# Gate and up weights of a pair of column blocks, read by depth halves in runs of 1 KB

## The chip, the core and the metric

The kernel runs on one core of one Trainium2 chip. The metric is the device time of one execution in microseconds (us), the median of three runs. The reference is float32 in and out.

## The reference

One layer of a decoder trunk, for a sequence of 1024 rows of width 1024. The change touches the two feed-forward blocks, one at the start and one at the end of the layer:

```python
def swiglu(h, w_gate, w_up, w_down):
    return (jax.nn.silu(h @ w_gate) * (h @ w_up)) @ w_down
...
x = x + 0.5 * swiglu(rms_norm(x, g_ffn1[l]), w1_gate[l], w1_up[l], w1_down[l])
h = rms_norm(x, g_mix[l])
proj = h @ w_in[l]
...   # two kinds of attention on proj, gates, an output projection added to x
x = x + 0.5 * swiglu(rms_norm(x, g_ffn2[l]), w2_gate[l], w2_up[l], w2_down[l])
```

`w_gate` and `w_up` are 1024 x 2816, `w_in` is 1024 x 4104, all float32. A row of a gate or up matrix is 11264 bytes.

## The kernel before, in words

**Tiling.** `ffn_in` computes gate and up for 22 column blocks of 128 columns, taken in 11 pairs `p`. For each pair the gate matrix (`e` = 0) and the up matrix (`e` = 1) each give a 256 x 1024 left side, cut into four quarters of 128 columns by 512 depth rows: A11, A12 (first block, first and second half of the depth), A21, A22 (second block). The first pair is multiplied directly (`opening`). Every later pair goes through seven products in place of eight (Strassen's scheme, `products`), so that four sums of quarters are formed first (`left_sides`: s1 to s4, on VectorE). Each left operand is then split into a rounded high part and a rest (`halve`: ScalarE copies to fp32r, GpSimd subtracts), and each product is twelve matmuls (`times`).

**Loads.** A load brings 512 KB into one `raw` tile of 128 partitions x 1024 float32. Before the change a load is one column block over the whole depth: 8 depth blocks x 128 columns, so each run in the weight matrix is 128 floats (512 bytes). The tile's first half is then A11 (or A21), its second half A12 (or A22). Four `raw` buffers go in turn: two for gate, two for up. The loads for a pair are issued as soon as the buffers of the pair before come free. In profile and order the tiles are `a0r` and `a1r` (gate and up of the first feed-forward block, the "a block") and `b0r`, `b1r` (of the last one, the "b block"); the high and low parts have names such as `a04A` and `a04S` (pair 4, gate).

**Work beside the a block.** While the a block runs, the kernel also splits columns of `w_in` into high and low parts for later: 48 pieces, each a load `swr` (256 KB, runs of 512 bytes, L799), a ScalarE copy `swh` (L789), a VectorE subtraction (L790) and two stores such as `wg14hd` and `wg14ld` (L793). Three pieces are under way at a time. `behind` ties each step of a piece to the end of one of the seven products, so that they follow TensorE's pace; their tiles are reused in turn, so that a new `swr` load waits for an older store to have landed. The b block has no such work beside it.

**What sets the order.** A scheduler puts the instructions of each engine in order when the program is built; VectorE's and ScalarE's instructions in `products` follow the products. All loads and stores here are issued by SyncE (SP) on one queue, in one order, and each waits until the eighth issue before it has landed (the waits on `DMAHW0` to `DMAHW7` below), besides the waits for its buffer.

**On ScalarE and VectorE** the steps of a piece stand in the same in-order queues as the steps that TensorE needs. In `products`, the accumulator `pd` is read by VectorE (L491, into `u3`) before the last product may add to it, and the accumulator `pa` of the next matrix is copied by ScalarE (L481) before it is added to. A piece's `swh` or subtraction that stands ahead of these in its queue and waits for a transfer holds them up.

Of the kernel before, what the change touches and what calls it, by code (L numbers as in the profile page):

```python
# [16 lines left out]
AF = mybir.ActivationFunctionType  # L17
# [40 lines left out]
def f32(ap):  # L58
    return ap.bitcast(F32)
# [186 lines left out]
def trunk(ctx, tc, x, positions, g_ffn1, w1_gate, w1_up, w1_down, g_mix, w_in, g_cq, w_uq_a, w_q_idx,  # L246
# [128 lines left out]
    def halve(t, src, eng=None):  # L375
# [2 lines left out]
        (eng or nc.gpsimd).tensor_tensor(t[:, LO], src, f32(t[:, HI]), op=ALU.subtract)  # L378
        return t

    class Right:


# [51 lines left out]
                nc.vector.tensor_sub(out[j], a[j], b[j])  # L435

    def loader(raw, nm):
        def load(w, f, name):
            t = raw(name)
            nc.sync.dma_start(t.rearrange("p (k f) -> p k f", k=ND),  # L440
                              w[0, :, f * P:(f + 1) * P].rearrange("(k p) f -> p k f", p=P))
            return t

        return load

    def ffn_in(nm, R, wg, wu, raw, op, sums, ct, bank, staged, rows, first=None, beside=lambda n, ins: None):

        B, load = R.B, loader(raw, nm)  # L450

        def left_sides(rs, name, pinned):
            A11, A12, A21, A22 = (r[:, q] for r in rs for q in (HI, LO))
            O = {n: op(f"{name}{n}") for n in ("A11", "S2", "S3", "S1", "A12", "A22", "S4")}
            s1, s2, s3, s4 = (sums(f"{name}s{n}") for n in range(1, 5))
            in_turn_ = tc.keep_in_program_order if pinned else lambda i: i
            in_turn_(nc.vector.tensor_add(s1, A21, A22))
            in_turn_(nc.vector.tensor_sub(s2, s1, A11))
            in_turn_(nc.vector.tensor_sub(s3, A11, A21))
            in_turn_(nc.vector.tensor_sub(s4, A12, s2))  # L460
            for n, src in (("A11", A11), ("S2", s2), ("S3", s3), ("S1", s1), ("A12", A12), ("A22", A22), ("S4", s4)):
                halve(O[n], src)
            return O

        def times(a, b, ps, start=True):
            for k in range(4):
                c, l = slice(k * P, (k + 1) * P), slice(512 + k * P, 512 + (k + 1) * P)
                nc.tensor.matmul(ps, a[:, c], b[k][:, HI], start=start and k == 0, stop=False, skip_group_check=True)  # L468
                nc.tensor.matmul(ps, a[:, c], b[k][:, LO], start=False, stop=False, skip_group_check=True)  # L469
                ins = nc.tensor.matmul(ps, a[:, l], b[k][:, HI], start=False, stop=k == 3, skip_group_check=True)  # L470
            return ins

        def mul(O, n, ps, start=True):
            a, b = FACTORS[n]
            beside("1675243".index(str(n)), times(O[a], B[b], ps, start))

        def products(O, name, nxt):
            pa = bank("pa", "a")
            mul(O, 1, pa)
            u2 = ct(f"{name}u2")  # L480
            nc.scalar.activation(u2, pa, AF.Copy)  # L481
            pb = bank("pb", "b")
            mul(O, 6, pb)
            nc.vector.tensor_add(u2, u2, pb)
            pc = bank("pc", "c")
            mul(O, 7, pc)
            u3 = ct(f"{name}u3")
            nc.vector.tensor_add(u3, u2, pc)
            pd = bank("pd", "d")
            mul(O, 5, pd)  # L490
            tc.keep_in_program_order(nc.vector.tensor_add(u3, u3, pd))  # L491
            nxt = nxt()
            mul(O, 2, pa, False)
            mul(O, 4, pc, False)
            c21 = ct(f"{name}c21")
            nc.vector.tensor_add(c21, u2, pc)
            mul(O, 3, pd, False)
            nc.vector.tensor_add(u2, u2, pd)
            return (pa, u2, c21, u3), nxt

        def opening(raws, rows, nxt):


            A = [dict(zip(("A11", "A12", "A21", "A22"), (r[:, q] for r in rs for q in (HI, LO)))) for rs in raws]
            O = ({}, {})

            def left(e, *names):
                for n in names:
                    O[e][n] = halve(op(f"{nm}{e}0{n}"), A[e][n])

            ps, sg = {}, {}

            def half(e, r, c, q):

                letter = "abcd"[r + 2 * c]
                if not q:
                    ps[e, r, c] = bank(f"p{letter}", letter)
                times(O[e][f"A{r + 1}{q + 1}"], B[f"B{q + 1}{c + 1}"], ps[e, r, c], not q)

            def gate(r, c):  # L520
                sg[r, c] = ct(f"{nm}sg")
                nc.scalar.activation(sg[r, c], ps[0, r, c], AF.Silu)

            def gated(r, c):
                nc.vector.tensor_mul(sg[r, c], sg[r, c], ps[1, r, c])

            if "B11" not in B:
                left(0, "A11")
                R.operand("B12")
                R.turn("B11")  # L530
                left(0, "A12")
                R.turn("B21")
                left(0, "A21", "A22")
                R.second()
            else:
                left(0, "A11", "A12", "A21", "A22")
            for t, n in enumerate(("A11", "A12", "A21", "A22")):
                if 4 - t <= len(rows):
                    R.stat(rows[t + len(rows) - 4])
                left(1, n)  # L540
            for t in rows:
                R.norm(t)
            half(0, 0, 0, 0)
            half(0, 0, 0, 1)
            gate(0, 0)
            half(0, 1, 0, 0)
            half(0, 1, 0, 1)
            gate(1, 0)
            half(1, 0, 0, 0)
            R.turn("B12", "cd")  # L550
            half(1, 0, 0, 1)
            R.sum("T1")
            gated(0, 0)
            R.turn("B22", "cd")
            half(1, 1, 0, 0)
            half(1, 1, 0, 1)
            gated(1, 0)
            half(0, 0, 1, 0)
            R.turn("T1", "ab")
            half(0, 0, 1, 1)  # L560
            gate(0, 1)
            R.sum("T2")
            half(0, 1, 1, 0)
            R.turn("T2", "ab")
            half(0, 1, 1, 1)
            gate(1, 1)
            R.sum("T4")
            R.sum("T3")
            half(1, 0, 1, 0)
            half(1, 0, 1, 1)  # L570
            R.turn("T3", "ab")
            gated(0, 1)
            nxt = nxt()
            half(1, 1, 1, 0)
            half(1, 1, 1, 1)
            R.turn("T4", "ab")
            gated(1, 1)
            return [sg[0, 0], sg[0, 1], sg[1, 0], sg[1, 1]], [ct(f"{nm}s{n}") for n in range(3)], nxt

        def silu(c):  # L580
            sg = ct(f"{nm}sg")
            nc.scalar.activation(sg, c[0], AF.Silu)
            for t in c[1:]:
                nc.scalar.activation(t, t, AF.Silu)  # L584
            return sg, *c[1:]

        def finish(p, H, S):
            (a11, a21, a12, a22), (s1, s2, s3) = H, S
            nc.vector.tensor_add(s1, a21, a22)
            nc.vector.tensor_sub(s2, s1, a11)  # L590
            nc.vector.tensor_sub(s3, a11, a21)
            nc.vector.tensor_sub(a21, a12, s2)
            for n, t in enumerate((a11, a12, a22, s1, s2, s3, a21)):
                nc.sync.dma_start(staged[p][n * P:(n + 1) * P, :], t)

        def lefts(p, e, pinned=False):
            if p == NF // 2:
                return None
            return left_sides([load((wg, wu)[e], 2 * p + q, f"{nm}{e}r{p}") for q in range(2)], f"{nm}{e}{p}", pinned)

        for p in range(NF // 2):
            if not p:
                first = first or [[load(w, q, f"{nm}{e}r0") for q in range(2)] for e, w in enumerate((wg, wu))]
                with tc.manual_schedule(engines={e.engine for e in (nc.tensor, nc.vector, nc.scalar, nc.gpsimd)}):
                    H, S, nxt = opening(first, rows, lambda: lefts(1, 0))
            else:
                for e, w in enumerate((wg, wu)):
                    u, nxt = products(nxt, f"{nm}{e}", lambda: lefts(p + e, 1 - e, True))
                    if not e:
                        H = silu(u)  # L610
                for a, b in zip(H, u):
                    nc.vector.tensor_mul(a, a, b)
                S = u[1:]
            finish(p, H, S)
# [147 lines left out]
    with tc.tile_pool(name="ring1", bufs=1) as rpool, tc.tile_pool(name="s1", bufs=1) as spool, tc.tile_pool(name="ps1", bufs=1, space=PSUM) as psum:  # L762
# [3 lines left out]
        with tc.tile_pool(name="t1", bufs=1, side="right") as tpool, tc.tile_pool(name="c1", bufs=1) as cpool:  # L766
# [40 lines left out]
            for t in range(4):  # L807
                rows(t)
                if t == 1:
                    R.gain()  # L810
            first = [[load(w, q, f"a{e}r0") for q in range(2)] for e, w in enumerate((w1_gate, w1_up))]
            for t in range(4, NT):
                rows(t)
            gcolm = column(g_mix, ND, "gcolm")
# [1358 lines left out]
```

## Time and profile before

| | us |
|---|---|
| median of three runs | 2239.9 (2239.87 to 2240.59) |
| profiled execution, its own time | 2240.86 |
| its span from the first to the last instruction | 2239.1 |
| TensorE busy | 2169.2 (97%) |
| VectorE busy | 1526.3 (68%) |
| ScalarE busy | 1104.4 (49%) |
| GpSimd busy | 858.2 (38%) |
| median from issue to landing, a0r and a1r (512 KB) | 6.7 and 7.2 |
| the same, b0r and b1r (512 KB) | 4.2 and 3.9 |
| the same, swr (256 KB) | 5.1 |

The mean granted clock of TensorE is 0.989 of full speed. The a block's steady pairs run from about 94 us to 460 us, those of the b block from about 1650 us to 1980 us. All times in traces are counted from the start of the span.

### The profile page before, as it was taken

The page shows a single profiled execution, that of the slowest core. Times are in us where ns is not written, and L with a number is a line of the kernel's source. Part 1 is how long each engine was busy: PE and PEld are TensorE (multiplying, and loading weights), DVE is VectorE, ACT ScalarE, POOL GpSimd, SP SyncE. Part 2 cuts the span into 40 slices and gives each one's busy share as a digit, 9 for nine tenths or more (in the row PEclk, how much of TensorE's full clock was granted, in tenths as well). Part 3 has the DMA queues.
Part 4 walks back from the last instruction along what each step waited for, and adds up shares of the span by engine and source line. Part 5 has one row for each costly group of instructions (what it writes and reads, how often), then busy time and mean ns, then how long its engine had stood idle before and what let it go on. Part 6 is the DMA issues. An engine that isn't in the chain of part 4 may idle for free.

```text
span 2239.1 us, 30578 instructions
## 1 busy us (share of the span) xinstructions
PE 2169.2 (97%) x10460; PEld 1807.1 (81%) x10460; DVE 1526.3 (68%) x2548; ACT 1104.4 (49%) x2169; POOL 858.2 (38%) x698
## 2 busy tenths in 40 slices
PE   7999999999999999899999899999999999999999
PEld 6887787788878988788788788877888888888877
DVE  5675675687875498677788688853465564668685
ACT  4333333334445258999989466533333232233443
POOL 3355455532236344211111322255245454552233
PEclk9999999999999999999999999999999999999999
DMA  5376676688686333665554623566223233349755
GB/s 171 99 216 199 205 239 190 195 286 275 198 219 177 111 118 126 195 176 170 151 160 164 209 95 99 170 218 236 67 77 117 90 113 97 115 160 324 229 165 184
DMA packets 269052, 381.01 MB, mean 170 GB/s; under 512 B 23264, under 2 KB 157040, under 8 KB 268896
## 3 DMA queue, kind: packets, MB, share of 16 engines
q1 hardware_dynamic: 256384, 339.17, 48.9%
q0 software_dynamic: 12512, 39.89, 4.9%
q8 instruction: 82, 1.34, 0.2%
q14 instruction: 74, 0.61, 0.1%
HBM read 259.94 MB, written 119.05 MB: 169 GB/s over the span
## 4 chain that ended last, share of the span: by engine, by line
PE 70%; ACT 7%; DVE 6%; DMA 4%; issue 3%; POOL 2%; SPq 0%; ACTq 0%; POOLq 0%; DVEq 0%
PE p L681 6%; PE p L682 6%; PE p L680 6%; ACT junka L1186 3%; PE pd L468 3%; PE pd L469 3%; PE pd L470 3%; PE pc L470 3%; PE pc L468 3%; PE pc L469 3%; PE pa L469 3%; PE pa L468 3%; PE pa L470 3%; PE psf L308 2%; PE psf L309 2%
## 5 line engine op out<-in xcount | busy, mean ns | idle before, releaser
L1186 ACT ACTIVATE junka<-u,cand,sig 128x768 bf16<-128x768 f32 (+4 forms) x186 | 183.8, 988 | 5.6 <-DVE cand L1183 4.0
L790 DVE TENSOR_TENSOR swr<-swr,swh 128x512 f32<-128x512 f32 x48 | 45.8, 954 | 111.2 <-ACT swh L789 107.2
L789 ACT ACTIVATE swh<-swr 128x512 fp32r<-128x512 f32 x48 | 30.2, 630 | 165.6 <-DMA swr<-in_w_in_dram 56.5
L1627 DVE TENSOR_TENSOR_SCAN left<-left 128x640 f32<-128x640 f32 (+3 forms) x64 | 86.3, 1349 | 4.0 <-ACT left L1619 4.0
L1120 POOL DMA_DIRECT2D gd<-evg x32 | 17.9, 560 | 152.6 <-ACT evg L1117 112.7
L1676 DVE TENSOR_TENSOR pt<-pstT,pt 128x512 fp32r<-128x512 f32 (+1 forms) x96 | 50.8, 549 | 28.6 <-ACT pt L1674 28.3
L584 ACT ACTIVATE b0u<-b0u 128x512 f32<-128x512 f32 x20 | 12.7, 633 | 95.3 <-DVE b0u L491 78.9
L1676 DVE TENSOR_TENSOR pt<-pspT,pt 128x512 fp32r<-128x512 f32 x72 | 46.8, 684 | 16.3 <-ACT pt L1674 16.3
L681 PE MATMUL p<-bT,bS 128*128 128x512 f32 x132 | 52.5, 398 | 2.4 <-DVE bT L378 2.4
L1674 ACT ACTIVATE pt<-pspT 128x512 fp32r<-128x512 f32 x72 | 39.7, 596 | 29.2 <-PE pspT L1886 29.1
L1807 ACT ACTIVATE e<-e,nm 128x256 f32<-128x256 f32 (+7 forms) x64 | 49.3, 773 | 9.3 <-DVE nm L1802 9.2
L1540 DVE SCALAR_TENSOR_TENSOR u<-relu,WI,u 128x512 f32<-128x512 f32 (+1 forms) x70 | 50.1, 733 | 5.2 <-ACT relu L1533 4.6
L1795 DVE CUSTOM_DVE_ANT_0 e<-psL,bias 128x512 f32<-128x512 f32 (+3 forms) x96 | 49.7, 550 | 5.5 <-PE psL L1832 5.5
L682 PE MATMUL p<-bT,bS 128*128 128x512 f32 x132 | 51.9, 396 | 1.0 <-POOL bS L378 1.0
L681 PE MATMUL p<-aT,aS 128*128 128x512 f32 x132 | 51.5, 390 | 0.0
L1630 DVE TENSOR_TENSOR sa<-sa,left 128x639 f32<-128x639 f32 (+3 forms) x64 | 48.1, 752 | 3.7 <-ACT sa L1621 0.2
L682 PE MATMUL p<-aT,aS 128*128 128x512 f32 x132 | 50.4, 389 | 0.0
L1674 ACT ACTIVATE pt<-pstT 128x512 fp32r<-128x512 f32 (+1 forms) x96 | 47.1, 519 | 3.3 <-PE pstT L1730 3.1
L1533 ACT ACTIVATE relu<-psdot 128x512 f32<-128x512 f32 (+1 forms) x80 | 40.1, 520 | 17.4 <-DVE u L1540 8.6
L1886 PE MATMUL pspT<-ident,e 128*128 128x128 f32 x288 | 39.6, 277 | 8.1 <-DVE ri L1809 5.5
L1619 ACT ACTIVATE left<-psz 128x512 f32<-128x512 f32 (+2 forms) x96 | 46.2, 505 | 2.0 <-PE psz L1654 1.8
L1621 ACT ACTIVATE sa<-psz 128x512 f32<-128x512 f32 (+2 forms) x96 | 47.0, 511 | 0.1
(3021 smaller groups left out, 8247.8 us busy)
## 6 DMA issues: line engine op xcount, KB each, us to landing
aw<-in_w_down_dram SPq DMA_DIRECT2D x33, 512.0 KB, 4.9
bw<-in_w_down_dram SPq DMA_DIRECT2D x33, 512.0 KB, 5.0
swr<-in_w_in_dram SPq DMA_DIRECT2D x48, 256.0 KB, 5.1
a0r<-in_w_gate_dram SPq DMA_DIRECT2D x22, 512.0 KB, 6.7
a1r<-in_w_up_dram SPq DMA_DIRECT2D x22, 512.0 KB, 7.2
b0r<-in_w_gate_dram SPq DMA_DIRECT2D x22, 512.0 KB, 4.2
b1r<-in_w_up_dram SPq DMA_DIRECT2D x22, 512.0 KB, 3.9
x<-in_x_dram SPq DMA_DIRECT2D x16, 512.0 KB, 6.1
```

Source lines behind the costliest of these rows:

```text
L468: nc.tensor.matmul(ps, a[:, c], b[k][:, HI], start=start and k == 0, stop=False, skip_group_check=True)
L469: nc.tensor.matmul(ps, a[:, c], b[k][:, LO], start=False, stop=False, skip_group_check=True)
L470: ins = nc.tensor.matmul(ps, a[:, l], b[k][:, HI], start=False, stop=k == 3, skip_group_check=True)
L680: nc.tensor.matmul(ps[q][m], S[:, h], T[:, HI], start=p == 0, stop=False)
L681: nc.tensor.matmul(ps[q][m], S[:, h], T[:, LO], start=False, stop=False)
L682: nc.tensor.matmul(ps[q][m], S[:, l], T[:, HI], start=False, stop=p == last)
L1186: nc.scalar.activation(junks[1][:, 0:(i + 1) * P], score[i], AF.Sign, scale=sig[:, b:b + 1], bias=cand.bitcast(F32)[:, b:b + 1], accum_out ...
L1540: nc.vector.scalar_tensor_tensor(ac, r, wv, ac, op0=ALU.mult, op1=ALU.add)
L1627: nc.vector.tensor_tensor_scan(back, back, back, 1.0, op0=ALU.mult, op1=ALU.bypass)
L1674: nc.scalar.activation(pt[:, off:512], tp[:, off:512], AF.Copy)
L1676: nc.vector.tensor_sub(pt[:, 512 + off:1024], tp[:, off:512], f32(pt[:, off:512]))
L1795: nc.vector.tensor_tensor_reduce(e[:, c], lp[:, 0:n_], bias[:, c], 1.0, LOW, op0=ALU.add, op1=ALU.max, accum_out=m)
```

## The change

Each of the two loads of a pair now brings one half of the depth of both column blocks: 4 depth blocks x 256 columns, so a run in the weight matrix is 256 floats (1 KB) and a load has 512 runs in place of 1024. The bytes are the same. In the tile, the columns of the two blocks now alternate in runs of 128, so a quarter is a strided view of 4 runs of 128 floats at a step of 256 (`quarters`), and the splits write their contiguous tiles through a view of the same form (`by_depth`, `quarter` in place of `halve`). The first tile (q = 0) now holds A11 and A21, the second (q = 1) A12 and A22. Number and sizes of the compute instructions are the same, and the order on TensorE, VectorE, ScalarE and GpSimd is the same, instruction by instruction.

```diff
+    def quarter(t, src):
+        nc.scalar.activation(by_depth(t[:, HI]), src, AF.Copy)
+        nc.gpsimd.tensor_tensor(by_depth(t[:, LO]), src, by_depth(f32(t[:, HI])), op=ALU.subtract)
+        return t
...
     def loader(raw, nm):
-        def load(w, f, name):
+        def load(w, p, q, name):
             t = raw(name)
-            nc.sync.dma_start(t.rearrange("p (k f) -> p k f", k=ND),
-                              w[0, :, f * P:(f + 1) * P].rearrange("(k p) f -> p k f", p=P))
+            nc.sync.dma_start(t.rearrange("p (k f) -> p k f", k=4),
+                              w[0, q * 512:q * 512 + 512, p * 2 * P:(p + 1) * 2 * P].rearrange("(k p) f -> p k f", p=P))
             return t
...
+    def quarters(rs):
+        t = [r.rearrange("p (k m f) -> p m k f", k=4, m=2) for r in rs]
+        return [t[q][:, m] for m in range(2) for q in range(2)]
+
+    def by_depth(a):
+        return a.rearrange("p (k f) -> p k f", k=4)
...
-            A11, A12, A21, A22 = (r[:, q] for r in rs for q in (HI, LO))
+            A11, A12, A21, A22 = quarters(rs)
...
-            s1, s2, s3, s4 = (sums(f"{name}s{n}") for n in range(1, 5))
+            s1, s2, s3, s4 = (by_depth(sums(f"{name}s{n}")) for n in range(1, 5))
...
-                halve(O[n], src)
+                quarter(O[n], src)
...
-            return left_sides([load((wg, wu)[e], 2 * p + q, f"{nm}{e}r{p}") for q in range(2)], f"{nm}{e}{p}", pinned)
+            return left_sides([load((wg, wu)[e], p, q, f"{nm}{e}r{p}") for q in range(2)], f"{nm}{e}{p}", pinned)
```

What moves is the order of issues on SP. The first place is the gate loads for pair 4 of the a block (`a0r4`, issued around 160 us before the change). `staged` are stores of the block's results, `swr` the loads of the work beside. Before:

```order
L594 DMA staged02_82<-a0u3_1212 128x512 [waits DMAHW1_49,DVE_49]
L594 DMA staged02_82<-asg_1312 128x512 [waits DMAHW2_49,DVE_49]
L799 DMA swr1_1448<-in_w_in_dram 128x4x128 [waits DMAHW3_49,DMAHW0_49,PE_49]
L793 DMA wg12hd_130<-swh2_1333 128x512 [waits DMAHW4_49,Activation_49]
L793 DMA wg12ld_131<-swr2_1332 128x512 [waits DVE_49]
L594 DMA staged02_82<-a0c21_1297 128x512 [waits DMAHW6_49,DVE_49]
L440 DMA a0r4_1713<-in_w1_gate_dram 128x8x128 [waits DMAHW7_49,Pool_49]
L440 DMA a0r4_1711<-in_w1_gate_dram 128x8x128 [waits Pool_49]
L594 DMA staged02_82<-a1u2_1335 128x512 [waits DMAHW1_49,DVE_49]
L799 DMA swr2_1498<-in_w_in_dram 128x4x128 [waits DMAHW2_49,PE_49]
```

After the change, the same stretch of SP's queue:

```order
L607 DMA staged02_82<-a0u3_1212 128x512 [waits DMAHW1_49,DVE_49]
L446 DMA a0r4_1711<-in_w1_gate_dram 128x4x256 [waits DMAHW2_49,DVE_49,Pool_49]
L607 DMA staged02_82<-asg_1312 128x512 [waits DMAHW3_49,DVE_49]
L812 DMA swr1_1448<-in_w_in_dram 128x4x128 [waits DMAHW4_49,DMAHW0_49,PE_49]
L806 DMA wg12hd_130<-swh2_1333 128x512 [waits Activation_49]
L806 DMA wg12ld_131<-swr2_1332 128x512 [waits DMAHW6_49,DVE_49]
L607 DMA staged02_82<-a0c21_1297 128x512 [waits DMAHW7_49,DVE_49]
L446 DMA a0r4_1713<-in_w1_gate_dram 128x4x256 [waits Pool_49]
L607 DMA staged02_82<-a1u2_1335 128x512 [waits DMAHW1_49,DVE_49]
L812 DMA swr2_1498<-in_w_in_dram 128x4x128 [waits DMAHW2_49,PE_49]
```

The first of the two loads stands five issues earlier; only one load is left ahead of the second `swr`. The first tile now comes free once s3 (VectorE) and the subtraction of A11 (GpSimd) are done, since A12 is no longer in it.

The second place is the up loads for the same pair (`a1r4`, issued around 181 us). Before:

```order
L793 DMA wg13ld_133<-swr1_1448 128x512 [waits DMAHW2_49,DVE_49]
L799 DMA swr1_1614<-in_w_in_dram 128x4x128 [waits DMAHW3_49,DMAHW2_49,PE_49]
L793 DMA wg14hd_134<-swh2_1499 128x512 [waits DMAHW4_49,Activation_49]
L793 DMA wg14ld_135<-swr2_1498 128x512 [waits DMAHW5_49,DVE_49]
L440 DMA a1r4_1879<-in_w1_up_dram 128x8x128 [waits DMAHW6_49,Pool_49]
L440 DMA a1r4_1877<-in_w1_up_dram 128x8x128 [waits Pool_49]
L799 DMA swr2_1654<-in_w_in_dram 128x4x128 [waits DMAHW1_49,DMAHW0_49,PE_49]
```

After the change:

```order
L806 DMA wg13ld_133<-swr1_1448 128x512 [waits DMAHW2_49,DVE_49]
L446 DMA a1r4_1877<-in_w1_up_dram 128x4x256 [waits DMAHW3_49,DVE_49,Pool_49]
L812 DMA swr1_1614<-in_w_in_dram 128x4x128 [waits DMAHW4_49,DMAHW2_49,PE_49]
L806 DMA wg14hd_134<-swh2_1499 128x512 [waits DMAHW5_49,Activation_49]
L806 DMA wg14ld_135<-swr2_1498 128x512 [waits DMAHW6_49,DVE_49]
L446 DMA a1r4_1879<-in_w1_up_dram 128x4x256 [waits Pool_49]
L812 DMA swr2_1654<-in_w_in_dram 128x4x128 [waits DMAHW1_49,DMAHW0_49,PE_49]
```

The first load of the pair is now ahead of a `swr` load and two stores that it stood behind; the second keeps its place. The same two moves recur in nearly every pair of the a block. In the b block the first gate load of a pair moves ahead in the same way, and nothing else.

More of the change, by code (lines that the diff above doesn't have):

```diff
@@ L501, in opening @@
         def opening(raws, rows, nxt):
-            A = [dict(zip(("A11", "A12", "A21", "A22"), (r[:, q] for r in rs for q in (HI, LO)))) for rs in raws]
+            A = [dict(zip(("A11", "A12", "A21", "A22"), quarters(rs))) for rs in raws]
             O = ({}, {})
@@ L508, in left @@
                 for n in names:
-                    O[e][n] = halve(op(f"{nm}{e}0{n}"), A[e][n])
+                    O[e][n] = quarter(op(f"{nm}{e}0{n}"), A[e][n])
             ps, sg = {}, {}
@@ L598, in lefts @@
                 return None
-            return left_sides([load((wg, wu)[e], 2 * p + q, f"{nm}{e}r{p}") for q in range(2)], f"{nm}{e}{p}", pinned)
+            return left_sides([load((wg, wu)[e], p, q, f"{nm}{e}r{p}") for q in range(2)], f"{nm}{e}{p}", pinned)
         for p in range(NF // 2):
             if not p:
-                first = first or [[load(w, q, f"{nm}{e}r0") for q in range(2)] for e, w in enumerate((wg, wu))]
+                first = first or [[load(w, 0, q, f"{nm}{e}r0") for q in range(2)] for e, w in enumerate((wg, wu))]
                 with tc.manual_schedule(engines={e.engine for e in (nc.tensor, nc.vector, nc.scalar, nc.gpsimd)}):
@@ L810, in trunk @@
                     R.gain()
-            first = [[load(w, q, f"a{e}r0") for q in range(2)] for e, w in enumerate((w1_gate, w1_up))]
+            first = [[load(w, 0, q, f"a{e}r0") for q in range(2)] for e, w in enumerate((w1_gate, w1_up))]
             for t in range(4, NT):
```

## The prediction

> **What bounds the kernel now.** I read the page first: TensorE is busy for nearly the whole span, so the change can only pay where TensorE waits or runs slow beside the gate and up loads. Next I cut the two feed-forward blocks into stretches of one pair each. The columns are the stretch, its length, busy time and count of instructions of TensorE, its weight loads, VectorE, ScalarE and GpSimd, the granted clock, DMA share and GB/s. The sum is over eight stretches of the a block from 94.3 to 420; the last row is one pair of the b block.
>
> ```profile
> 173.90:215.70 41.80, 39.86 (x175) 32.15 (x174) 26.32 (x32) 15.15 (x29) 22.15 (x16) 1.00 0.71 208
> 215.70:260.30 44.60, 38.28 (x154) 30.68 (x153) 25.53 (x32) 13.84 (x27) 19.54 (x14) 0.92 0.67 194
> 337.60:382.10 44.50, 40.12 (x166) 32.61 (x165) 25.57 (x33) 14.42 (x28) 22.26 (x16) 0.92 0.67 196
> sum 325.70, PE 311.86 PEld 254.86 DVE 206.89 ACT 112.63 POOL 168.07; mean PE 38.98 PEld 31.86 DVE 25.86 ACT 14.08 POOL 21.01
> 1693.70:1731.80 38.10, 38.10 (x170) 31.55 (x169) 21.16 (x27) 11.12 (x21) 19.95 (x15) 1.00 0.33 104
> ```
>
> A pair takes 38.1 us in the b block, with TensorE busy throughout and DMA at a third. There the loads are hidden and the change is worth nothing. In the a block eight pairs take 325.7 us against 8 x 38.1 = 304.8: 20.9 us lie there to be won, under 1%. The waits of TensorE (60:200, then 200:250, 350:400, 400:520; total, times, longest) say where:
>
> ```profile
> PE pd L468 <- DVE a1u L491: 1.8, 1, 1.8
> PE pb L470 <- POOL a04S L378: 0.2, 1, 0.2
> PE pa L468 <- ACT a1u L481: 3.3, 1, 3.3
> PE pd L468 <- DVE a1u L491: 3.0, 1, 3.0
> PE pd L468 <- DVE a1u L491: 5.2, 2, 4.4
> PE pc L470 <- POOL a09S L378: 0.4, 1, 0.4
> ```
>
> They sum to 13.9 us. The two stretches with clock 0.92 lose another 0.08 x 44.6 + 0.08 x 44.5 = 7.1 us to TensorE's lower clock. Together 21.0, which is all of the excess. Four places: A near 187 (1.8 and 0.2), C from 222 to 240 (3.3, 3.0 and 3.6 of clock), D at 357 (4.4 and 3.6 of clock), E near 400 (0.8 and 0.4).
>
> Who is late there? The timeline around D, SP's issues first (start, length of issue), then the three engines behind them:
>
> ```profile
> 338.65 0.38 SPq L799 DMA_DIRECT2D swr<-in_w_in_dram  x1
> 339.68 0.38 SPq L793 DMA_DIRECT2D wqk10320ld<-swr  x1
> 344.81 0.38 SPq L799 DMA_DIRECT2D swr<-in_w_in_dram  x1
> 345.84 0.38 SPq L793 DMA_DIRECT2D wqk5201ld<-swr  x1
> 346.31 1.19 SPq L440 DMA_DIRECT2D a1r<-in_w_up_dram  x2
> 347.61 7.03 SPq L799 DMA_DIRECT2D swr<-in_w_in_dram  x1
> ...
> 354.74 0.63 ACT L789 ACTIVATE swh<-swr 128x512 fp32r<-128x512 f32 x1 [10.06 <-DMA wqk5201ld<-swr]
> ...
> 355.40 0.69 DVE L790 TENSOR_TENSOR swr<-swr,swh 128x512 f32<-128x512 f32 x1 [9.09 <-ACT swh L789]
> ...
> 356.74 0.79 PE L468 MATMUL pd<-aB,a17S 128*128 128x512 f32 x1 [4.38 <-DVE a1u L491]
> ```
>
> TensorE waits for VectorE's L491, queued behind the piece's subtraction L790, which waits for ScalarE's `swh`, which waits for a store issued at 345.84 to land at about 354.7. So the bound in these places is the latency of the work beside, a loop of load, copy, subtraction, store and the next load. Not the weight loads themselves: no wait of TensorE ends with one. They matter as traffic in the same queue.
>
> **The change part by part.** *Strided quarters.* ScalarE, VectorE and GpSimd now read 4 runs of 128 floats. The trace has such shapes already, with 4 runs of 128 (L1515 writes, L1517 reads and writes) and 4 runs of 256 (L1300 reads). The columns are min/median/max in ns; the last row is GpSimd's contiguous 128x512 subtraction.
>
> ```profile
> L1515 ACT ACTIVATE qsi<-psqt x12: 588/594/596, 774.3 to 867.6; 64x512 fp32r<-64x512 f32 x12
> L1517 DVE TENSOR_TENSOR qsi<-psqt,qsi x12: 683/688/694, 777.5 to 868.3; 64x512 fp32r<-64x512 f32 x12
> L1300 POOL TENSOR_TENSOR wka0l<-wka0r,wka0h x1: 2410/2410/2410, 712.7 to 712.7; 128x1024 fp32r<-128x1024 f32 x1
> L378 POOL TENSOR_TENSOR a13A<-a1r,a13A x3: 1285/1731/1810, 159.7 to 175.5; 128x512 fp32r<-128x512 f32 x3
> ```
>
> Half of 2410 is 1205 ns for 512 elements, against 1285 contiguous; VectorE's 688 is the 690 of L790 in D, ScalarE's 594 is under the 630 of `swh`. Cost: nothing. ScalarE and VectorE also have idle time here (13.84 and 25.53 us busy of 44.60); were a run to cost 0.05 us more, 7 splits x 2 matrices x 0.05 = 0.7 us a pair would still be covered.
>
> *Shorter transfers.* The rate of 512-byte runs shows when only gate and up loads are moving, at 10.5 to 15 us; that of 4 KB rows, when only x is, at 17.5 to 21:
>
> ```profile
> 10.50:15.00 4.50, 0.45 (x1) 0.18 (x1) 3.19 (x5) 1.44 (x3) 2.33 (x3) 1.00 1.22 291
> 17.50:21.00 3.50, 3.50 (x26) 3.28 (x25) 2.93 (x6) 3.31 (x7) 1.30 (x1) 1.00 1.03 410
> ```
>
> A load is 524,288 bytes: 1.80 us at 291 GB/s. With 1 KB runs it lies between 1.80 and 1.28 us (410 GB/s). I take the middle, 1.54: a gain of 0.26 us a load, 1.0 us a pair. The Trainium skill ("DMA: Bandwidth & Descriptors", Specifications) puts the smallest transfer at line rate at 512 bytes. By that rule the 0.26 is nothing: C below would gain nothing, A and E would still gain by the moved load, and the sum would be 3.3 in place of 4.8 us. The two rows differ by 29%, so above 512 bytes something is still to be had.
>
> *The moved load.* Each pair's first load goes ahead of one `swr` load. It adds no instruction, but a wait for its buffer ahead of queued issues. For the up load near 181, s3 stands just ahead of s4 on VectorE, and A11's subtraction is the first of the three in the row `a13A` above (159.7):
>
> ```profile
> 169.43 0.68 DVE L460 TENSOR_TENSOR a13s<-a1r,a13s 128x512 f32<-128x512 f32 x1
> 181.20 1.34 SPq L440 DMA_DIRECT2D a1r<-in_w_up_dram  x2
> ```
>
> The buffer is free at about 169.4 and the new place comes at about 176.3, behind the store that precedes the next `swr` (174.81 in the next fence, plus two stores). No wait; and until that `swr` at 179.70 there are 3.4 us, which hide 0.4 us of issue and 1.54 us of transfer. What comes out from behind the pair gains 1.80 + 0.26 = 2.06 us. How that reaches A:
>
> ```profile
> 160.59 1.56 SPq L440 DMA_DIRECT2D a0r<-in_w_gate_dram  x2
> 162.24 3.23 SPq L594 DMA_DIRECT2D staged<-a1u  x1
> 165.56 0.39 SPq L799 DMA_DIRECT2D swr<-in_w_in_dram  x1
> ...
> 174.81 0.38 SPq L799 DMA_DIRECT2D swr<-in_w_in_dram  x1
> ...
> 179.70 0.38 SPq L799 DMA_DIRECT2D swr<-in_w_in_dram  x1
> ...
> SPq L799 <- DMA wg13ld<-swr: 8.5, 2, 5.0
> ...
> 186.84 0.63 ACT L789 ACTIVATE swh<-swr 128x512 fp32r<-128x512 f32 x1 [6.92 <-DMA wg14ld<-swr]
> ```
>
> The pair at 160.59 clogs the queue (3.23 us to issue one store). The `swr` and the stores of `wg13` behind it land late, the two `swr` loads at 174.81 and 179.70 both wait for those stores, and that ends in the late `swh` at 186.84. Taking 2.06 us off the head covers A's 1.8 + 0.2: -2.0 (bounds 0 and -2.0).
>
> *E* I price like A, its pairs too standing ahead: -0.8 (bounds 0 and -1.2).
>
> *C* starts differently:
>
> ```profile
> 202.45 0.45 SPq L440 DMA_DIRECT2D a0r<-in_w_gate_dram  x1
> ...
> 204.14 0.44 SPq L799 DMA_DIRECT2D swr<-in_w_in_dram  x1
> ...
> 216.28 0.38 SPq L799 DMA_DIRECT2D swr<-in_w_in_dram  x1
> ...
> SPq L799 <- DMA wg0ld<-swr: 15.7, 2, 7.9
> ```
>
> Here the two gate loads are already apart (the issue at 202.45 is x1), and still the loop is late. Only the shorter packets are left, 0.26 for each of two loads in front: 0.5 off each wait, with 0.5 for the clock: -1.5 (bounds 0 and -9.9). The Trainium skill ("TensorE: Matmul & The Clock Gate", Part 1) says that about 3.4 us without work halve the clock. Rows agree (1.8 us left it at 1.00, 3.3 did not), and by that rule a wait cut to 2.8 would save the whole 1.8 us of its slow spell.
>
> *D* starts from a `swr` at 338.65 that has no pair near it. The 8.9 us landing at 345.84 has the up loads behind it, not ahead; one goes away from there. I take -0.5 (bounds +1.8, for a load now ahead of it, and -8.0).
>
> The b block, the opening (the second weight tile is wanted earlier, but has landed long before) and the rest: 0. Sum: -2.0 - 0.8 - 1.5 - 0.5 = -4.8. The profiled execution took 2240.86 us, 0.96 above the median, so 2236.1 there and about 2235 as a median.
>
> **The rivals.** *No gain that shows.* A change of under 0.2% (4.5 us) can't be told from none here. The latency of a `swr` load may not hang on the traffic ahead at all. Of the 48 loads at L799:
>
> ```profile
> DMA to landing us min/median/max: 3.5/5.1/13.8
> ```
>
> These 256 KB take 3.5 to 13.8 us, and the load at 344.81 was slow with an empty queue. If the slow ones stay slow, A alone shrinks: 2238 to 2240. *A large gain.* If it is the bunching of two loads that makes neighbours slow (the issue of 7.03 us at 347.61 stands right behind a pair), C and D collapse too: 2239.9 - 2.8 - 0.75 x 17.9 = 2224. *Slower.* The up load that now stands between a store and the next `swr` delays that `swr`. The place is D and its like; the price is up to 1.8 us a pair, plus 3.6 us where a wait newly reaches 3.3 us; it decides once the gap ahead of the `swr` (3.4 us at 179.70, about 4.7 at 344.81) is under the load's time in the queue, which takes a queue already 2 us behind. Two such pairs and one slow spell give 2239.9 + 3.6 + 3.6 = 2247. C speaks for it (loads apart, worst loop), A's chain against it.
>
> **How the numbers follow.** Forecast case (A and E go, C and D hardly): 0.45, at 2235, own range 2231 to 2239, a little over half of it faster by more than 0.2%. Large gain: 0.24. No change: 0.22. Slower: 0.09. Faster 0.24 + 0.25 = 0.49, same 0.22 + 0.20 = 0.42, slower 0.09. The range 2221 to 2243 takes in the large gain with some spread below 2224, and leaves out most of the slower case.
>
> **What would show it.** Right: split and sum rows within 3% of today's; median landing of a0r and a1r down from 6.7 and 7.2 to about 5; no issue of 3 to 7 us behind a1r; A's wait gone, and 43 to 45 us still in the stretches of C and D. Wrong: strided rows that take longer; the waits at C or D gone, or new waits in pairs that have none now, with SP held at a gate or up load.

## The result, and the profile after

| | before | after |
|---|---|---|
| median, us | 2239.9 (6 runs, 2237.29 to 2240.59) | 2223.2 (6 runs, 2221.36 to 2227.41) |
| profiled execution, its own time | 2240.86 | 2223.29 |
| its span | 2239.1 | 2221.5 |
| mean granted clock of TensorE | 0.989 | 0.992 |

The ratio is 0.993, with a 95% interval of 0.9918 to 0.9943: 16 us faster, well over the 0.2% that a measurement can tell. Times and ratios, here and below, are of fast executions; one of the kernel before, beside runs 10 to 12, took 3616.93 us at a granted clock of 0.56 and is left out. The work is the same. The page of after has for TensorE (the row of before said 2169.2):

```profile
PE 2160.5 (97%) x10460; PEld 1802.0 (81%) x10460; DVE 1528.6 (69%) x2548; ACT 1104.2 (50%) x2169; POOL 862.0 (39%) x698
```

The same 10460 matmuls, 8.7 us less busy time (6.2 of it in the eight pairs below, where less of the work ran at the lower clock), and the rest of the gain is waits that are gone. Where, is best read by cutting the a block at the first matmul of each pair's gate products. Eight pairs, before (stretch, length, busy time and count of TensorE, its weight loads, VectorE, ScalarE and GpSimd, granted clock, DMA share, GB/s):

```profile
151.50:191.70 40.20, 38.42 (x169) 31.46 (x169) 24.24 (x30) 14.48 (x26) 21.11 (x15) 1.00 0.72 214
191.70:240.50 48.80, 42.33 (x170) 33.53 (x169) 27.60 (x36) 15.58 (x29) 21.62 (x16) 0.93 0.64 180
...
316.70:362.00 45.30, 40.92 (x169) 33.10 (x168) 26.41 (x33) 14.96 (x28) 23.33 (x16) 0.93 0.68 192
362.00:401.50 39.50, 38.73 (x169) 31.70 (x168) 24.82 (x31) 13.33 (x25) 18.59 (x14) 0.99 0.70 220
401.50:440.30 38.80, 38.37 (x169) 31.45 (x168) 26.49 (x33) 15.17 (x29) 25.33 (x18) 1.00 0.57 183
sum 326.80, PE 312.96 PEld 255.80 DVE 206.49 ACT 114.39 POOL 172.23; mean PE 39.12 PEld 31.98 DVE 25.81 ACT 14.30 POOL 21.53
```

The same pairs after:

```profile
151.80:189.90 38.10, 38.10 (x170) 31.54 (x169) 26.52 (x31) 14.87 (x27) 23.62 (x16) 1.00 0.76 239
189.90:234.10 44.20, 39.82 (x169) 32.51 (x168) 24.13 (x33) 12.81 (x24) 18.22 (x14) 0.96 0.64 186
...
310.30:348.40 38.10, 38.10 (x170) 31.56 (x169) 25.34 (x32) 14.36 (x26) 20.97 (x15) 1.00 0.68 191
...
sum 311.10, PE 306.72 PEld 253.23 DVE 208.73 ACT 115.82 POOL 175.64; mean PE 38.34 PEld 31.65 DVE 26.09 ACT 14.48 POOL 21.95
```

Eight pairs took 326.8 us and now take 311.1, against 8 x 38.1 = 304.8 with nothing in the way. So 15.7 of the 17.6 us between the two spans lie here. A (40.2) and D (45.3) are down to 38.1, E's two pairs too. C alone is left, at 44.2. All waits of TensorE from 60 to 470 us are now one row, and the timeline shows what stands ahead of it:

```profile
PE pd L481 <- DVE a1u L504: 4.4, 1, 4.4
```

```profile
227.79 0.63 ACT L802 ACTIVATE swh<-swr 128x512 fp32r<-128x512 f32 x1 [9.40 <-DMA wg1ld<-swr]
228.45 0.69 DVE L803 TENSOR_TENSOR swr<-swr,swh 128x512 f32<-128x512 f32 x1 [8.45 <-ACT swh L802]
229.06 0.68 DVE L504 TENSOR_TENSOR a1u<-a1u,pd 128x512 f32<-128x512 f32 x1
229.79 0.79 PE L481 MATMUL pd<-aB,a14S 128*128 128x512 f32 x1 [4.38 <-DVE a1u L504]
```

It is the chain of before: a transfer of the work beside that lands late, its copy, its subtraction, VectorE's `u3`, TensorE.

The rows that answer to the terms of the prediction are the rate at 10.5 to 15 us (291 before), the splits and the third sum, and the landings of `a0r` (first) and `a1r` (second):

```profile
10.50:15.00 4.50, 0.45 (x1) 0.18 (x1) 3.24 (x5) 1.39 (x3) 2.33 (x3) 1.00 1.09 351
```

```profile
L383 ACT ACTIVATE a13A<-a1r x3: 612/617/617, 151.6 to 168.3; 128x512 fp32r<-128x512 f32 x3
L384 POOL TENSOR_TENSOR a13A<-a1r,a13A x3: 1284/1284/1734, 158.8 to 172.2; 128x512 fp32r<-128x512 f32 x3
```

```profile
L472 DVE TENSOR_TENSOR a13s<-a1r x1: 685/685/685, 165.6 to 165.6; 128x512 f32<-128x512 f32 x1
```

```profile
DMA to landing us min/median/max: 3.7/6.0/9.5
```

```profile
DMA to landing us min/median/max: 3.7/6.2/10.7
```

And the 48 loads of the work beside, issue first (min/median/max in ns), then landing:

```profile
L812 SPq DMA_DIRECT2D swr<-in_w_in_dram x48: 367/384/712, 81.0 to 389.2; - x48
DMA to landing us min/median/max: 3.5/5.7/12.2
```

The longest issue of a `swr` load was 7.03 us and is 0.71. The slowest landing was 13.8 and is 12.2, the median even rose from 5.1 to 5.7: the slow loads stayed slow, and yet C's waits are 4.4 us in place of 6.3, and D's is gone.

### The profile page after: what moved, and what is told of

It reads as the page before. It is cut to its first block, busy times and chain, and to the rows that moved or that the text cites. A ratio compares the mean times of both kernels' runs of the same rounds, so it can differ in the third digit from the quotient of the medians.

```text
span 2221.5 us, 30587 instructions
## 1 busy us (share of the span) xinstructions
PE 2160.5 (97%) x10460; PEld 1802.0 (81%) x10460; DVE 1528.6 (69%) x2548; ACT 1104.2 (50%) x2169; POOL 862.0 (39%) x698
## 4 chain that ended last, share of the span: by engine, by line
PE 75%; DVE 8%; ACT 8%; DMA 4%; issue 3%; POOL 1%; SPq 0%; ACTq 0%; DVEq 0%; POOLq 0%
PE p L694 5%; PE p L695 5%; PE p L693 5%; ACT junka L1199 4%; PE pd L481 3%; PE pd L482 3%; PE pd L483 3%; PE pc L481 3%; PE pc L482 3%; PE pc L483 3%; PE pa L482 3%; PE pa L481 3%; PE pa L483 3%; PE psf L308 2%; PE psf L309 2%
```

## The experiments

Two questions: which half of the change does it, the order of the loads or the longer runs; and why do the waits go when the slow `swr` loads stay? My theory after the result, "lead": the loop of load, split, store and next load, three pieces at a time, has a few us of lead on TensorE. Whatever delays it is carried from piece to piece, and TensorE waits only where the lead is used up. Rivals: each wait has its own local cause ("local"), or the pairs of loads make it alone ("pair", "packets"). The time of before is that of the same chip in each row; the gain is 1 less the ratio, times 2240.

| run | what differs | us | before | ratio (95%) | gain |
|---|---|---|---|---|---|
| 1 | after's order, runs of 512 B, two transfers a tile | 2225.1 | 2240.6 | 0.9928 (0.9916 to 0.9941) | 16.1 |
| 2 | the same with runs of 1 KB | 2225.4 | 2240.6 | 0.9930 (0.9918 to 0.9942) | 15.7 |
| 3 | runs of 1 KB, loads of a pair together | 2234.0 | 2240.6 | 0.9968 (0.9956 to 0.9980) | 7.2 |
| 4 | after, pieces in reverse order | 2224.0 | 2240.6 | 0.9921 (0.9908 to 0.9934) | 17.7 |
| 5 | before, without the slow loads | 2225.8 | 2238.5 | 0.9939 (0.9926 to 0.9951) | 13.7 |
| 6 | after, without the slow loads | 2218.9 | 2238.5 | 0.9910 (0.9896 to 0.9924) | 20.2 |
| 7 | after, slow pieces nine apart | 2220.4 | 2238.5 | 0.9917 (0.9903 to 0.9930) | 18.6 |
| 8 | after, slow pieces in a row | 2228.0 | 2239.5 | 0.9951 (0.9937 to 0.9964) | 11.0 |
| 9 | after, wg1 last | 2219.3 | 2238.5 | 0.9909 (0.9895 to 0.9922) | 20.4 |
| 10 | the change in the b block alone | 2239.6 | 2240.3 | 0.9999 (0.9990 to 1.0007) | 0.2 |
| 11 | after, again | 2223.9 | 2240.3 | 0.9931 (0.9915 to 0.9947) | 15.5 |
| 12 | wg1 last, again, beside 11 | 2219.4 | 2240.3 | 0.9908 (0.9893 to 0.9923) | 20.6 |

### Order or packets: runs 1, 2 and 3

Run 1 keeps the tiles by depth halves, with each tile filled by one transfer for each column block:

```diff
-            nc.sync.dma_start(t.rearrange("p (k f) -> p k f", k=4),
-                              w[0, q * 512:q * 512 + 512, p * 2 * P:(p + 1) * 2 * P]...)
+            for m in range(2):
+                nc.sync.dma_start(t[:, m * 512:m * 512 + 512].rearrange("p (k f) -> p k f", k=4),
+                                  w[0, q * 512:q * 512 + 512, (2 * p + m) * P:(2 * p + m + 1) * P]...)
```

> The new order without the 1 KB runs: tiles hold depth halves as in the changed kernel, so the first load of a pair is released early and stands ahead of one `swr` load, but each tile is filled by two transfers of 256 KB with runs of 512 bytes. That is one more issue of about 0.4 us on SP a tile. Theory 'order' (the gain comes from the first load standing apart from the second): about 2224 us, 14 to 18 us under the kernel before, and no issue of 3 to 7 us on SP. Theory 'packets' (the gain comes from half as many packets in the queue): 2237 to 2243, landing of a0r and a1r near 7 us, waits of TensorE between 60 and 460 us still above 10 us in sum, and issues of 3 us and more on SP. My own split in the prediction (2.06 us a moved load, of which 0.26 from the runs) says mostly order.

Run 2 has two transfers a tile as well, but of two depth blocks and both columns each, in runs of 1 KB:

> Control for the run before: the changed kernel with each tile filled by two transfers of 256 KB, but with runs of 1 KB. Order of issues and number of issues as in that run. If the extra issue costs nothing, 2221 to 2227 us, as the changed kernel. If it takes SP's time that the loop of load, split and store needs, up to 2230; then the run before is to be read against this one.

Run 3 makes the first load of a pair wait for the last reader that its buffer had before the change (`after`, GpSimd's subtraction of the previous pair's A12):

```diff
+            if after is not None:
+                tc.add_manual_dep(dma.ins, after.ins.name, ...)
```

> The 1 KB runs without the new order: the changed kernel, but the first load of each pair also waits for the GpSimd subtraction of A12, as the kernel before did through its buffer. The loads of a pair stand together on SP again (those of pair 6 too, which were apart before; some `swr` loads come two issues later). Theory 'order': 2235 to 2243 us, issues of 3 to 7 us behind pairs remain. Theory 'packets': 2221 to 2229, rate of a lone load 350 GB/s, no issue over 2 us behind a pair, and the waits of TensorE between 60 and 460 us under 8 us in sum.

Run 1 gives the whole gain with the old runs: 16.1 us, as run 2 and the change. Its rate at the start is the old one, those of runs 2 and 3 are the new one:

```profile
10.50:15.00 4.50, 0.45 (x1) 0.18 (x1) 2.27 (x5) 1.36 (x3) 2.79 (x3) 1.00 1.22 292
```

```profile
10.50:15.00 4.50, 0.45 (x1) 0.18 (x1) 3.24 (x5) 1.38 (x3) 2.33 (x3) 1.00 1.10 351
10.50:15.00 4.50, 0.64 (x2) 0.18 (x1) 3.17 (x6) 1.78 (x3) 2.33 (x3) 1.00 1.09 355
```

Run 3 fell between the theories: 7.2 us, with waits of TensorE of 10.1 us in sum left (13.9 before). So either half helps, order more, and their gains do not add: 16.1 + 7.2 would be 23.3, more than lies there to be won. What both do is to unclog SP. Its longest issue of a `swr` load, of run 1 and of run 3:

```profile
L813 SPq DMA_DIRECT2D swr<-in_w_in_dram x48: 367/384/1336, 81.9 to 390.0; - x48
```

```profile
L819 SPq DMA_DIRECT2D swr<-in_w_in_dram x48: 367/384/1466, 81.4 to 401.2; - x48
```

Counted over SP's timeline from 30 to 470 us, issues of over 1.4 us are 21 with 63.0 us in sum before, 2 with 5.3 in run 1, 4 with 7.7 in run 2, 5 with 10.1 in run 3, 3 with 6.2 after. A pair before was 2048 runs in a row. A lone tile of 512-byte runs and a pair of 1 KB tiles are 1024 each, and neither clogs SP in that way.

### Which loads are slow: run 4

In both profiles three of the 24 columns are slow in both their loads: wg9 (9.8 and 12.2 us after), wg1 (9.3 and 7.5) and wqk10321 (7.8 and 12.2). Of the other 42 loads after, 41 took 3.5 to 7.7 us; the second of wg2, close behind wg1's, took 10.0. Before, four more took 8.1 to 10.5, each right behind a pair of up loads. Run 4 reverses the list of columns (`for nm in reversed(columns)`).

> The changed kernel with the columns of the work beside taken in the reverse order (same loads, splits and stores). In both profiles so far the `swr` loads of three columns (wg9 at 92 to 95 us, wg1 at 197 to 217, wqk10321 at 330 to 348) are the slow ones, 7.5 to 13.8 us; these columns are 4096 bytes apart in a row of w_in. Theory 'address' (a slow load goes with its column): slow loads now near 140 us (wqk10321), 256 to 262 (wg1) and 373 to 380 (wg9), and 3.5 to 7 us at 92, 197 and 330; the wait of 4.4 us at 225 goes, or moves to one of the new places; 2218 to 2227 us. Theory 'place' (a slow load goes with the traffic at its time): slow loads stay at 92, 197 to 221 and 330, the wait stays at 225, the time stays at 2221 to 2227.

"Address" held for the three columns. Issues and landings in run 4 around 92, 132 and 372 us:

```profile
L812 SPq DMA_DIRECT2D swr<-in_w_in_dram x2: 367/367/367, 92.2 to 94.9; - x2
DMA to landing us min/median/max: 4.9/5.2/5.5
```

```profile
L812 SPq DMA_DIRECT2D swr<-in_w_in_dram x2: 384/384/384, 132.1 to 135.7; - x2
DMA to landing us min/median/max: 8.2/9.3/10.4
```

```profile
L812 SPq DMA_DIRECT2D swr<-in_w_in_dram x2: 383/450/517, 372.0 to 375.0; - x2
DMA to landing us min/median/max: 7.8/9.9/12.1
```

At 92 us, where wg9 took 9.8 and 12.2 after, another column now takes 4.9 and 5.5. wqk10321 took its slowness along to 132, wg9 to 372, and wg1 to 262 and 271 (7.9 and 8.0). The wait moved too: 3.4 us at 302, behind wg1 and the two columns after it (wg0, wg15). But the column is not all: four loads of others took 8.1 to 9.9 us in run 4 (at 250, 274, 298 and 353). wg9, wg1 and wqk10321 lie 4096 bytes apart in a row of `w_in`. Why they are slow was not found out.

### Slow loads and clogged pairs: runs 5 and 6

In both kernels those six loads read the neighbour's column:

```diff
                         nm, c = pieces.pop(0)
+                        at = columns[nm] + P * (nm in ("wg9", "wg1", "wqk10321"))
...
-                                                      rows_of[:, c // P:(c + 512) // P, columns[nm]:columns[nm] + P]))
+                                                      rows_of[:, c // P:(c + 512) // P, at:at + P]))
```

> The kernel before, with the six slow `swr` loads taken away: wg9, wg1 and wqk10321 are read 128 columns further on (the columns of their neighbours), so those three columns of the work beside are wrong in the output; everything else is the same. Theory 'lead' (the loop of load, split and store has a few us of lead on TensorE; slow columns and clogged pairs both eat it, and TensorE waits only where it is used up): C and D vanish with their slow clock, 2240.6 - 15 to 18 = 2222 to 2226 us; A and E (1.8 + 0.2, 0.8 + 0.4) may stay. Theory 'pair' (two loads in a row are enough to make C and D): C and D keep at least 8 of their 17.9 us, 2232 or more. Theory of the prediction (C and D are mostly the slow loads themselves): as 'lead'.

> The changed kernel, with the same six loads read 128 columns further on (those three columns of the work beside are wrong in the output). Theory 'lead': the wait of 4.4 us at 225 and its slow clock go and no other comes, 2223.2 - 5 to 7 = 2216 to 2218 us. If the wait came from the block's own loads, it stays and the time is 2221 to 2225.

Run 6 has no wait of TensorE at all between 60 and 470 us. The time of 2218.9 is a little over the 2216 to 2218 expected. Run 5 took away 13.7 us from before, less than the 15 to 18 expected, and D did not vanish. Its wait there, and its longest `swr` issue, behind the up loads as before:

```profile
PE pd L468 <- DVE a1u L491: 3.1, 1, 3.1
```

```profile
L800 SPq DMA_DIRECT2D swr<-in_w_in_dram x48: 367/384/5392, 81.3 to 392.6; - x48
```

So D is mostly the pairs' doing, C (1.3 us of wait left in run 5) mostly the slow columns'. The two causes do not add either (13.7 alone, 15.5 for the change alone, 20.2 together).

How late the loop is at D can be read off directly: from the start of pair 7's first up product (`a17A`, its first weight load) to the issue of the `swr` load that the split behind it needs. Before (the load was at 344.81), run 5, run 2, run 3, run 1, after; for runs 2 and 3 with that load's landing:

```profile
335.66 0.19 PEld L468 LDWEIGHTS pa<-aB,a17A 128*128 128x128 f32 x1
```

```profile
326.47 0.19 PEld L468 LDWEIGHTS pa<-aB,a17A 128*128 128x128 f32 x1
335.78 0.38 SPq L800 DMA_DIRECT2D swr<-in_w_in_dram  x1
```

```profile
326.38 0.19 PEld L483 LDWEIGHTS pa<-aB,a17A 128*128 128x128 f32 x1
331.56 0.37 SPq L814 DMA_DIRECT2D swr<-in_w_in_dram  x1
DMA to landing us min/median/max: 9.1/9.1/9.1
```

```profile
332.90 0.19 PEld L488 LDWEIGHTS pa<-aB,a17A 128*128 128x128 f32 x1
338.08 0.38 SPq L819 DMA_DIRECT2D swr<-in_w_in_dram  x1
DMA to landing us min/median/max: 7.9/7.9/7.9
```

```profile
326.00 0.19 PEld L482 LDWEIGHTS pa<-aB,a17A 128*128 128x128 f32 x1
330.70 0.37 SPq L813 DMA_DIRECT2D swr<-in_w_in_dram  x1
```

```profile
329.11 0.19 PEld L481 LDWEIGHTS pa<-aB,a17A 128*128 128x128 f32 x1
330.02 0.38 SPq L812 DMA_DIRECT2D swr<-in_w_in_dram  x1
```

Runs 2 and 3 are both 5.2 us late, and yet run 2 waits 1.0 us at D and run 3 does not: run 2's load took longer to land. So the landing belongs in the count:

| | issue late by, us | landing after | sum | wait at D |
|---|---|---|---|---|
| before | 9.2 | 8.5 | 17.7 | 4.4 |
| run 5 | 9.3 | 7.0 | 16.3 | 3.1 |
| run 2 | 5.2 | 9.1 | 14.3 | 1.0 |
| run 3 | 5.2 | 7.9 | 13.0 | none |
| run 1 | 4.7 | 7.6 | 12.3 | none |
| after | 0.9 | 7.8 | 8.7 | none |

Each wait is what the sum has over 13.3 us, and sums below that cost nothing. That is the lead. A before (9.3 and 5.7, wait 1.8) and C after (9.9 and 7.7, wait 4.4) fit the same 13.3 within 0.2 us. A late issue and a slow landing count alike. In run 5 this load was of a fast column and TensorE waited nonetheless; after, it was of a slow one (the next landed only 12.2 us after its issue) and TensorE did not.

### Spread or bunched: runs 7 and 8

Run 7 puts the six slow pieces at places 2, 11, 20, 29, 38 and 47, run 8 at 18 to 23:

```diff
+            slow = [s for s in pieces if s[0] in ("wg9", "wg1", "wqk10321")]
+            pieces = [s for s in pieces if s not in slow]
+            for n, s in enumerate(slow):        # run 7
+                pieces.insert(2 + 9 * n, s)
+            pieces[18:18] = slow                # run 8, in place of the loop
```

> The changed kernel with the same work, but the six slow pieces stand nine apart in the order (places 2, 11, 20, 29, 38 and 47) in place of two at a time. Theory 'lead': a slow load alone (8 to 9 us against 5.7) is covered, the wait of 4.4 us goes, 2216 to 2219 us. If each slow load costs its excess wherever it stands, waits of 1 to 2 us come at several places and the time stays at 2221 to 2226. If the second of two slow loads (10 to 13 us) is slow because of the first, all six now take 7 to 9 us.

> The changed kernel with the same work, but the six slow pieces (wg9, wg1, wqk10321) stand in a row at places 18 to 23, near 197 to 240 us. Theory 'lead': lateness adds up in the loop, so with nothing fast between them the waits near 225 to 245 come to 10 us or more, no wait stands anywhere else, and the time is 2228 to 2238 us, against 2220.4 for the same six pieces nine apart. Theory 'local' (a slow load costs what it costs where it stands): the same sum as two at a time, 2221 to 2227.

Run 7 came 1.4 us over its range, and its waits are 0.5, 0.4 and 0.4. Five of its six slow loads took 7.6 to 9.7 us, one 5.4: the landings over 12 us of after were each the second of two in a row. The load right behind a slow one was slow too, though of a fast column: 7.5 to 9.3 us at all five places. Run 8, with the same loads, gains 7.6 us less than run 7, and its waits all stand between 220 and 255:

```profile
PE pd L481 <- DVE a0u L504: 4.4, 1, 4.4
PE pd L481 <- DVE a1u L504: 2.2, 1, 2.2
```

"Lead" had said 10 us and more of waits and 2228 to 2238; it is 6.6 us and 2228.0, at the very edge. The sign and the place are right; the lateness adds up less than I thought. "Local" (2227 at most) is out by 1 us only, so run 8 alone decides little; against run 7 it is clear.

### One slow column moved to the end: runs 9, 11 and 12

```diff
+            pieces.sort(key=lambda s: s[0] == "wg1")
```

> The changed kernel with only the two pieces of wg1 moved to the end of the order, behind wqk10323 (issues near 384 and 390). Theory 'lead': the wait at 225 goes; wqk10321 now comes two places earlier, near 315, where 3 to 5 us of lead were left; 2216 to 2219 us. If wg1 brings its wait along to 395, 2221 to 2225.

> The changed kernel itself, on the same chip as the next run, so that the two can be compared: 2221 to 2226 us.

> The changed kernel with the two pieces of wg1 last, a second time, beside the changed kernel. With no wait of TensorE left in the a block but one of 0.3 us, it should be 3 to 6 us under the changed kernel on the same chip: 2217 to 2220 us. Were the reordering worth nothing, 2222 to 2225.

The wait at 225 is gone in both. Run 9 has 0.2 us of wait left from 60 to 470, at 127. Run 12, the same kernel, has one of 2.2 us near 397, behind the subtraction of wg1's second piece, which took 7.9 us to land:

```profile
398.15 0.69 DVE L804 TENSOR_TENSOR swr<-swr,swh 128x512 f32<-128x512 f32 x1 [4.88 <-ACT swh L803]
399.50 0.50 PE L481 MATMUL pd<-aB,a09S 128*128 128x512 f32 x1 [2.17 <-DVE a0u L504]
```

So in that execution wg1 brought half of its wait along to the end. Each run has one profile, and a wait of 2 us comes and goes between executions of one kernel.

2219.3 and 2219.4 us (8 runs, 2217.5 to 2221.95), against 2223.9 for the changed kernel on the chip of run 12 (6 runs, 2220.63 to 2229.62). That is 4.5 us, about the bound of 0.2%; the intervals of the two ratios overlap a little, so the gain is likely and not proven.

### The b block: run 10

The loader, the quarters and the splits are the old ones where `nm == "a"`.

> The change in the b block alone: the a block loads by column blocks and splits contiguous quarters as before, the b block loads depth halves in runs of 1 KB. The prediction put the b block at 0. If that holds: 2237 to 2242 us, the same as before, and the stretch of one b pair stays at 38.1 us. If part of the 17 us came from there: 2235 or less.

The ratio is 0.9999, and one pair of the b block takes what it took, 38.1 us with TensorE busy throughout:

```profile
1698.70:1736.80 38.10, 38.10 (x170) 31.55 (x169) 21.14 (x26) 11.11 (x20) 19.94 (x15) 1.00 0.34 104
```

## Why the prediction was right and where it was not

The time of 2223.2 lies in the range, near its lower end, and the direction was the likeliest one. But the forecast case (2235) is not what came. It was the rival "large gain", at 2224, to which I had given 0.24. The range held because its lower end was set for that rival; the sum missed by 12 us.

- **What bounds the kernel.** Right. The pot of 20.9 us is what the versions with hardly a wait left gain (20.2 to 20.6 us), and the work beside is what TensorE waits for.
- **Strided quarters, 0.** Right: 617, 1284 and 685 ns against 617, 1285 (least) and 684. **The b block, 0.** Right (run 10).
- **Shorter transfers, 0.26 us a load.** Right in size: at 351 GB/s a load takes 1.49 us where I took 1.54, so 0.31. The Trainium skill ("DMA: Bandwidth & Descriptors", Specifications) puts line rate at 512 bytes; the rows 292 and 351 of runs 1 and 2, which differ in the runs alone, disagree.
- **A, -2.0.** Right in size: the stretch went from 40.2 to 38.1. But the pair ahead was not its only cause. A's wait (and E's) is gone in run 5 too, where the pairs stayed and wg9's loads near 92 became fast. **E, -0.8** (bounds 0 and -1.2): 39.5 and 38.8 went to 38.1 and 38.0, which is 2.2, outside the bounds. The waits there sum to 1.2 us only, and I had bounded E by them, not by the two stretches, which were 2.1 us over 2 x 38.1.
- **C, -1.5.** The stretch went from 48.8 to 44.2: -4.6, inside the bounds (0 and -9.9). **D, -0.5.** 45.3 to 38.1: -7.2, near the far bound (-8.0). These two terms are 9.8 us short, and the forecast was 12 us too high by the medians.
- **The step that failed** is "D starts from a `swr` at 338.65 that has no pair near it", and its like for C ("only the shorter packets are left"). I priced each place by what stands next to it in the queue. But that load was late itself. SP's waits from 334 to 346 show that it and the next one, at 344.81, each stood until a store of an older piece had landed:

```profile
SPq L799 <- DMA wqk10320ld<-swr: 9.9, 2, 5.2
```

So lateness passes from piece to piece, back to the pairs and the slow columns before. The rows were at hand: the `swr` that D waits for was issued 9.2 us behind the start of its product, and is issued 0.9 us behind it after. That is 8.3 us, where I had counted 2.06 us for a moved load and only at A and E. By this reading D also got what the loop had gained before it; how much came from which place was not measured.
- **The rival "large gain"** had the right cause for the wrong reason. Run 1 shows that taking the loads apart is enough. But the neighbours hardly became fast: the six `swr` loads that stood right behind a pair of up loads before (at 143, 183, 229, 269, 309 and 348) land 0.5 to 2.1 us sooner behind their issue after the change, and those of the three columns stayed slow. For the rival "no gain" I argued that if the slow loads stay slow, A alone shrinks. They stayed slow, and C and D shrank.
- **The rival "slower"** did not show: after, an up load at 331.48 stands just ahead of the `swr` at 332.25, and no pair that had no wait got one.
- **What would show it.** Landings came down to 6.0 and 6.2, not to 5; run 3's, with both loads together, stayed at 6.6 and 7.2, so this is the order's work. C's stretch is still at 44.2, as I had said. D's wait is gone, and that I had named as a sign of being wrong.

Of the 17.6 us between the profiles, 1.9 lie outside the eight pairs. Run 10 leaves no room for the b block in it; I did not trace it further, and executions of one kernel differ by more (6 us after).

## What to carry to other kernels

Where work beside runs as a loop with its own latency (load, copy, store, buffer free, load), don't price a change at the places where the bottleneck engine waits. Measure how far the loop is behind the engine at each turn, find what delays it anywhere upstream, and expect delays to add up until the lead is gone; the gains of several cures then overlap (here 16.1, 7.2 and 13.7 us alone, 20.6 at most). Pricing every wait by its neighbours gave too little here. And sort the slow turns of such a loop to where there is lead left, or to its end: that was one line and about 4.5 us here, with one wait of 2.2 us that came along.

## What the runs showed of the hardware

- **Slow columns.** 256 KB in 512 runs of 512 bytes from `w_in` (row pitch 16416 bytes) landed after 3.5 to 7.7 us in 41 of 42 cases after, but after 7.6 to 9.7 us alone (five of six in run 7), and up to 12.2 after and 13.8 before as the second in a row, for three columns that start 544 bytes behind a multiple of 4096 in the first row. Columns that start 32 or 1056 behind one are not slow by themselves (wg10, 5.0 and 6.9 us after; wg2, 6.8 and 6.4 in run 9, where wg1 no longer stands ahead of it). It went with the column when the order was reversed. The cause is open.
- **SP clogs on many runs in a row.** Behind 2048 runs of 512 bytes the next issue took up to 7.03 us in place of 0.38. With 1024 runs in a row (runs 1 and 3) a `swr` issue took 1.5 us at most, and the longest store issue was 3.7 us (3.8 in run 11, the changed kernel again).
- **The clock.** A wait of 2.18 us was enough to halve TensorE's clock in run 8 (its row below, and the stretch behind it at 0.53), while one of 2.17 in run 12 was not; in run 3 a wait of 2.57 halved it and one of 2.98 did not (the last two stretches, 0.58 and 1.00):

```profile
227.46 0.79 PE L481 MATMUL pd<-aB,a14S 128*128 128x512 f32 x1 [2.18 <-DVE a1u L504]
```

```profile
227.60:231.00 3.40, 3.40 (x9) 2.68 (x10) 3.40 (x6) 1.75 (x4) 1.05 (x1) 0.53 0.63 161
```

```profile
223.00:226.00 3.00, 3.00 (x9) 2.36 (x8) 1.17 (x2) 0.00 (x0) 0.00 (x0) 0.58 0.37 77
392.50:396.00 3.50, 3.50 (x16) 2.88 (x17) 3.42 (x6) 1.85 (x4) 1.14 (x1) 1.00 0.51 176
```

The Trainium skill ("TensorE: Matmul & The Clock Gate", Part 1) asks for an idle window of about 3.4 us, free-running. That the same wait now halves the clock and now does not fits a free-running window; that 2.18 us suffice does not fit a window that must be idle throughout. The clock records of all fourteen traces show more: the granted clock changes only on a grid of 3.41 us that runs on through waits. Cut along that grid, every interval with 2 us or more of TensorE idle halved a full clock, and none with 1.4 or less did; between these it went either way. Run 8's wait has 2.1 us in one interval and run 3's 2.57 lies in one, while run 3's 2.98 is split into 1.3 and 1.7. In the prediction I read the rule as a threshold on the wait; a wait of 2 to 3 us can cost another 1.6 us (3.4 us at 0.53) or nothing.
